# Finishing each differential head inside the next one: root, norm and turn behind the second tile

## The chip, the core and the metric

The kernel runs on one core of a Trainium2 chip. The metric is the device time of one execution in microseconds (us). Three runs of the kernel before took 1695.03, 1695.44 and 1698.78 us; the median is 1695.44. A further execution was profiled: it took 1692.59 us, of which the span of the trace covers 1690.8. All rows below are of that execution.

The engines are named as in the profile: PE is TensorE (matrix products and transposes), DVE is VectorE, ACT is ScalarE, POOL is GpSimd, SP is SyncE, which issues DMAs. Each works through its own queue of instructions.

## The reference

An encoder of two layers over 512 tokens of width 1024. Each layer has a mixer, a cross attention to 256 memory tokens and a mixture of sixteen experts, each followed by a residual and a layer norm. The mixer of the first layer is differential attention with eight heads; the change lies there:

```python
def differential_attention(x, cos, sin, w_in, lam, subln_g, w_out, lambda_init):
    h, d = DIFF_HEADS, DIFF_HEAD_DIM            # 8, 64
    q, k, v = jnp.split(x @ w_in, 3, axis=-1)
    # q, k: rope, then (seq, h, 2, d); v: (seq, h, 2 * d)
    s = jnp.einsum('bqhcd,bkhcd->bhcqk', q_blk, k)
    p = jax.nn.softmax(jnp.where(allowed, s, -jnp.inf), axis=-1)
    p_diff = p[:, :, 0] - lam_full * p[:, :, 1]
    o = jnp.einsum('bhqk,bkhe->bqhe', p_diff, v)
    o = rms_norm(o, subln_g) * (1.0 - lambda_init)
    return o.reshape(bsz, seq, h * 2 * d) @ w_out

def rms_norm(x, g):
    return x * lax.rsqrt(jnp.mean(x * x, axis=-1, keepdims=True) + LN_EPS) * g
```

A token sees the keys of its own and earlier chunks of 64. The norm is taken per token and head, over the head's 128 output columns.

## The kernel before, in words

Everything stays on one core. Weights stream from memory through a ring of buffers and are split into a high part and the rest (ScalarE writes the high part at L203 or, scaled, L207; VectorE the rest at L204 or L208). A projection is three products per chunk of 128 (`mm3`, L248 to L250).

The first mixer is a function with local helpers. `qk_proj(h)` makes queries and keys of head h: 48 products into two PSUM tiles pq, rope into two SBUF tiles qk, and for each of these two groups of four transposes, which the text calls turns: qp and kp (L430). The turned queries are evacuated to qab by ScalarE and VectorE (L253, L254), the turned keys to kS (L439, L440). `v_proj(g)` makes the values of two heads. `mem_kv(h)` makes keys and values of the memory for one head of the cross attention (mk, mv); its first call loads the memory into two tiles (L532, issued by SP) and turns it (mT, L535). These two tiles come from the same ring of two buffers as the qk tiles.

`attend(h)` goes over four tiles of 128 queries. For each: scores sc for both components (L466), mask and maximum on VectorE (L468 to L471), exponentials on ScalarE (L475), reciprocal and difference on VectorE (L478 to L481), transposes pT of the difference (L485), their copy pTs (L487), the value product po (L490). ScalarE scales po into og and, with a second pass, sums its squares into ssq (L491, L492). After the fourth tile `attend` finishes the head: twelve small VectorE instructions for the reciprocal root of ssq (`rsqrt`, L187 to L196), the scaling of og (L495), four transposes oT (L498), and the evacuation: a copy to oF for heads 0 to 5, high part and rest for heads 6 and 7 (L501, L502). When attend(6) is done, the six copies are split as well. The output projection (op0o) takes oTh and oTl.

The turns pT, qp, kp and oT and the products po share a PSUM pool of two buffers ("tp"); pq, pv, mk and mv share another of two; the scores and mT a third of two.

The driver calls qk_proj(0), v_proj(0), qk_proj(1), and then for each head attend(h) followed by the entries of a table:

```python
FILL = [["q2"], ["v1", "q3"], ["q4"], ["v2", "q5"], ["m0", "q6"], ["v3", "q7"], ["m1", "m2"], ["m3"]]
```

The order of the program text is not the order on the engines. A scheduler at build time orders the instructions of PE, DVE and ACT by its own estimate of when each could start; buffers of a pool are handed out in the order of the program text, so a turn that the text names earlier takes its buffer earlier. SP's and POOL's queues follow the text. In the result the scores of head h+1 run ahead of the end of head h, and the turns of head h+2 follow it.

At the end of the first MoE layer, ACT, DVE and the others test a register for further blocks of tokens (the branch of L1082; the trace has one such test per layer and engine, and no further block). Behind it the last expert's product is evacuated (byh, byl, L253, L254), added (mhx, L1238), and the layer norm begins (L303), which needs its gain, mg (L1221). ACT also splits weights for the second layer there, among them bwqih (L207).

Of the kernel before, what the change touches and what calls it, by code (L numbers as in the profile page):

```python
# [18 lines left out]
ALU = mybir.AluOpType  # L19
# [3 lines left out]
P = 128  # L23
D = 1024
S = 512
NT = S // P
# [3 lines left out]
EPS = 1e-5  # L30
# [35 lines left out]
def encoder(ctx: ExitStack, tc: tile.TileContext, I, out):  # L66
    nc = tc.nc
# [8 lines left out]
    def tp(name):  # L76
        return ps.tile([P, 512], F32, tag="tp", name=name, bufs=2)

    def sc2(name):
        return ps.tile([P, 1024], F32, tag="sc", name=name, bufs=2)  # L80
# [3 lines left out]
    def t4(tag, name, shape=None, dtype=F32):  # L84
        return sb.tile(shape or [P, 1024], dtype, tag=tag, name=name, bufs=BUFS[tag])

    def t2(tag, name, shape=None, dtype=F32):
        return sb.tile(shape or [P, 512], dtype, tag=tag, name=name, bufs=BUFS[tag])
# [17 lines left out]
    def small(name, shape, dtype=F32, bufs=2):  # L106
        return sb.tile(shape, dtype, tag="_" + re.sub(r"\d+", "", name), name=name, bufs=bufs)
# [4 lines left out]
    ident = const.tile([P, P], F32, name="ident")  # L112
# [70 lines left out]
    def rsqrt(x, n, name, mul, add, room=None):  # L183

        v, y, w, yi = (small(f"rs{q}{name}", [P, room or n], I32 if q == "i" else F32)[:, 0:n] for q in "vywi")
        k = 2.0 ** 26
        nc.vector.tensor_scalar(v, x, mul * k, add * k, op0=ALU.mult, op1=ALU.add)  # L187
        nc.vector.tensor_scalar(yi, v.bitcast(I32), 1, None, op0=ALU.logical_shift_right)  # L188
        nc.vector.tensor_scalar(y.bitcast(I32), yi, -1, 0x5F3759DF - 2 ** 31, op0=ALU.mult, op1=ALU.add)  # L189
        for c in (3.0, 12.0, 768.0):  # L190
            if n == 1:
                nc.vector.scalar_tensor_tensor(w, y, v, y, op0=ALU.mult, op1=ALU.mult)
            else:
                nc.vector.tensor_tensor(w, y, y, op=ALU.mult)  # L194
                nc.vector.tensor_tensor(w, w, v, op=ALU.mult)  # L195
            nc.vector.scalar_tensor_tensor(y, w, -c, y, op0=ALU.add, op1=ALU.mult)  # L196
        return y
# [44 lines left out]
    def ts(t):  # L242
        return slice(t * P, (t + 1) * P)
# [8 lines left out]
    def split_evac(hi, lo, src):  # L252
        nc.scalar.activation(hi, src, AF.Copy)  # L253
        nc.vector.tensor_sub(lo, src, hi.bitcast(F32))  # L254
# [105 lines left out]
    def diff_attention(x_ap):  # L360
# [25 lines left out]
        oF = Tall("oF", F32)  # L386
        oT = []
# [54 lines left out]
        def v_proj(g):  # L442
            W = U.get(f"wv{g}")
            vs[g] = t4("b", f"V{g}", [P, NT, 256])
            for th in range(2):
# [4 lines left out]
                        [(hT[0](k, c), hT[1](k, c), W[0][:, k, :], W[1][:, k, :]) for k in range(8)])  # L450
                nc.any.tensor_copy(vs[g][:, 2 * th:2 * th + 2, :], pv.rearrange("p (u n) -> p u n", u=2))

        def attend(h):
            V = vs[h // 2][:, :, ts(h % 2)]
            qab, K = QAB[h % 2], kS[h]
            og = t2("g", f"og{h}", [P, NT, P])
            ssq = small(f"ssq{h}", [P, NT])
            for t in range(NT):
                n = (t + 1) * P
                c = ts(t)  # L460
                nm = f"{h}{t}"
                sc = sc2(f"sc{nm}").rearrange("p (c n) -> p c n", c=2)
                w = max(n, 256)
                for cc in range(2):
                    for v in range(2):
                        nc.tensor.matmul(sc[:, cc, 0:w], qab[:, 2 * v + cc, c], K[:, cc, 0:w],  # L466
                                         start=v == 0, stop=v == 1)
                nc.vector.memset(sc[0:CHUNK, :, n - CHUNK:n], NEG)  # L468
                mx = small(f"mx{nm}", [P, 2])
                nc.vector.tensor_reduce(mx, sc[:, :, 0:n], axis=AX.X, op=ALU.max)  # L470
                nc.vector.tensor_scalar(mx, mx, -0.125, None, op0=ALU.mult)  # L471
                sm = small(f"sm{nm}", [P, 2])
                p_ = t4("c", f"p{nm}", [P, 2, 512])
                for cc in range(2):
                    nc.scalar.activation(p_[:, cc, 0:n], sc[:, cc, 0:n], AF.Exp, bias=mx[:, cc:cc + 1],  # L475
                                         scale=0.125, accum_out=sm[:, cc:cc + 1])
                rs = small(f"rs{nm}", [P, 2])
                nc.vector.reciprocal(rs, sm)  # L478
                c1 = small(f"c1{nm}", [P, 1])
                nc.vector.scalar_tensor_tensor(c1, sm[:, 0:1], rs[:, 1:2], nlam, op0=ALU.mult, op1=ALU.mult)  # L480
                nc.vector.scalar_tensor_tensor(p_[:, 0, 0:n], p_[:, 1, 0:n], c1, p_[:, 0, 0:n],  # L481
                                               op0=ALU.mult, op1=ALU.add)
                pt = tp(f"pT{nm}")
                for kt in range(t + 1):
                    nc.tensor.transpose(pt[:, ts(kt)], p_[:, 0, ts(kt)], ident)  # L485
                pT = t2("f", f"pTs{nm}")
                nc.any.tensor_copy(pT[:, 0:n], pt[:, 0:n])  # L487
                po = tp(f"po{nm}")
                for kt in range(t + 1):
                    nc.tensor.matmul(po[:, 0:P], pT[:, ts(kt)], V[:, kt, :], start=kt == 0, stop=kt == t)  # L490
                nc.scalar.activation(og[:, t, :], po[:, 0:P], AF.Copy, scale=rs[:, 0:1])  # L491
                nc.scalar.activation(junk[:, 0:P], po[:, 0:P], AF.Square, scale=rs[:, 0:1],  # L492
                                     accum_out=ssq[:, t:t + 1])
            rstd = rsqrt(ssq, NT, f"rms{h}", 1.0 / P, EPS)
            nc.vector.tensor_tensor(og, og, rstd.unsqueeze(2).to_broadcast([P, NT, P]), op=ALU.mult)  # L495
            pt = tp(f"oT{h}")
            for t in range(NT):
                nc.tensor.transpose(pt[:, ts(t)], og[:, t, :], ident)  # L498
            if oT:
                split_evac(oT[0](h), oT[1](h), pt)  # L500
            else:  # L501
                nc.any.tensor_copy(oF(h), pt)  # L502

        qk_proj(0)
        v_proj(0)
        qk_proj(1)
        for h in range(8):
            attend(h)
            if h == 6:
                for k in range(6):  # L510
                    split_evac(oT[0](k), oT[1](k), oF(k))
            for f in FILL[h]:
                if f[0] == "m":
                    mem_kv(int(f[1]))
                else:
                    (qk_proj if f[0] == "q" else v_proj)(int(f[1]))
            if h == 5:
                oT.extend((Tall("oTh"), Tall("oTl")))
        return tuple(oT)


# [1045 lines left out]
    x_ap = I["x"][0]  # L1567
    h2_d = dr.tile([S, D], F32, name="h2_d")
    oT = diff_attention(x_ap)
    nl = 2  # L1570
    for i in range(nl):
# [8 lines left out]
        oT, begun = mem_attention(i, hT)  # L1580
# [40 lines left out]
        if i + 1 < nl:  # L1621
            D3[0](DSA)
            oT = tuple(D3[1])
# [27 lines left out]
```

## Time and profile before

| what | us |
|---|---|
| runs shown, median (lowest to highest) | 1695.44 (1695.03 to 1698.78) |
| profiled execution | 1692.59 |
| its span | 1690.8 |
| PE busy in the span | 1522.3 (90%) |
| DVE busy | 1206.2 (71%) |
| ACT busy | 862.6 (51%) |

Busy time of an engine is the time in which at least one of its instructions ran. In a timeline row the first number is the start from the span's beginning, the second the duration; a bracket at the end holds the idle time of the engine ahead of it and what ended that. Matrix products are pipelined, so the duration of one reaches over the start of the next. Heads are not written in the names of a timeline; they follow from the order: the eight rows of oT at L498 are heads 0 to 7, at 100.81, 131.83, 164.67, 184.09, 212.22, 271.98, 311.54 and 330.37 us.

### The profile page before, as it was taken

The page shows a single profiled execution, that of the slowest core. Times are in us where ns is not written, and L with a number is a line of the kernel's source. Part 1 is how long each engine was busy: PE and PEld are TensorE (multiplying, and loading weights), DVE is VectorE, ACT ScalarE, POOL GpSimd, SP SyncE. Part 2 cuts the span into 40 slices and gives each one's busy share as a digit, 9 for nine tenths or more (in the row PEclk, how much of TensorE's full clock was granted, in tenths as well). Part 3 has the DMA queues.
Part 4 walks back from the last instruction along what each step waited for, and adds up shares of the span by engine and source line. Part 5 has one row for each costly group of instructions (what it writes and reads, how often), then busy time and mean ns, then how long its engine had stood idle before and what let it go on. Part 6 is the DMA issues. An engine that isn't in the chain of part 4 may idle for free. (4 is left out here: it accounts for less than half of the span.)

```text
span 1690.8 us, 23295 instructions
## 1 busy us (share of the span) xinstructions
PE 1522.3 (90%) x8572; PEld 1292.7 (76%) x8572; DVE 1206.2 (71%) x2381; ACT 862.6 (51%) x1156; POOL 230.2 (14%) x228
## 2 busy tenths in 40 slices
PE   7998799698995899999996899998998699999994
PEld 7988699597784777888875757698777487888883
DVE  5555746555447998898875698836436899899795
ACT  5443646432320775775763454533322477677671
POOL 1000000011004031231210000002002222132120
PEclk9999899799996899999997999999998699999998
DMA  7210234432415798998974301024242599899883
GB/s 227 75 51 1 75 113 157 156 91 87 165 59 213 246 364 314 311 355 314 320 254 157 96 25 63 26 89 151 76 142 110 211 363 371 281 333 368 280 300 124
DMA packets 118334, 317.58 MB, mean 188 GB/s; under 512 B 23773, under 2 KB 72925, under 8 KB 93632
## 3 DMA queue, kind: packets, MB, share of 16 engines
q1 hardware_dynamic: 100400, 272.00, 45.3%
q0 software_dynamic: 17808, 43.96, 8.5%
q8 instruction: 71, 1.16, 0.3%
q14 instruction: 55, 0.45, 0.1%
HBM read 299.38 MB, written 36.70 MB: 199 GB/s over the span
## 5 line engine op out<-in xcount | busy, mean ns | idle before, releaser
L204 DVE TENSOR_TENSOR cell_l<-cell_r,cell_h 128x2048 fp32r<-128x2048 f32 x192 | 430.7, 2285 | 40.4 <-ACT cell_h L203 39.9
L203 ACT ACTIVATE cell_h<-cell_r 128x2048 fp32r<-128x2048 f32 x192 | 363.4, 1915 | 77.7 <-DMA cell_r<-in_moe_w_up_dram 17.8
L954 PE MATMUL pg<-cell_h,xh 128*128 128x512 f32 x288 | 118.9, 413 | 2.2 <-ACT xh L253 2.2
L982 PE MATMUL py<-cell_h,hsh 128*128 128x512 f32 x288 | 115.4, 401 | 1.4 <-ACT hsh L253 0.7
L954 PE MATMUL pg<-cell_l,xh 128*128 128x512 f32 x288 | 116.2, 403 | 0.0
L982 PE MATMUL py<-cell_h,hsl 128*128 128x512 f32 x288 | 112.8, 392 | 0.0
L982 PE MATMUL py<-cell_l,hsh 128*128 128x512 f32 x288 | 112.5, 390 | 0.0
L954 PE MATMUL pu<-cell_h,xh 128*128 128x512 f32 x288 | 112.0, 389 | 0.0
L954 PE MATMUL pu<-cell_l,xh 128*128 128x512 f32 x288 | 112.0, 389 | 0.0
L972 POOL DMA_INDIRECT acc_d<-y,sx x34 | 72.9, 2143 | 152.1 <-ACT y L971 103.2
L932 POOL DMA_INDIRECT xg<-h_d,sx x32 | 42.0, 1312 | 363.8 <-DVE sx L919 334.2
L253 ACT ACTIVATE xh<-xgT 128x1024 fp32r<-128x1024 f32 x36 | 36.9, 1024 | 101.6 <-PE xgT L939 95.9
L954 PE MATMUL pg<-cell_h,xl 128*128 128x512 f32 x288 | 79.8, 400 | 0.0
L954 PE MATMUL pu<-cell_h,xl 128*128 128x512 f32 x288 | 77.0, 389 | 0.0
L954 PEld LDWEIGHTS pg<-cell_h,xh 128*128 128x128 f32 x288 | 56.6, 197 | 14.1 <-ACT xh L253 3.0
L954 PEld LDWEIGHTS pg<-cell_h,xl 128*128 128x128 f32 x288 | 56.1, 195 | 12.5
L954 PEld LDWEIGHTS pg<-cell_l,xh 128*128 128x128 f32 x288 | 56.3, 195 | 11.4
L982 PEld LDWEIGHTS py<-cell_h,hsh 128*128 128x128 f32 x288 | 54.2, 188 | 13.0 <-DVE xl L254 1.0
L982 PEld LDWEIGHTS py<-cell_h,hsl 128*128 128x128 f32 x288 | 54.0, 188 | 12.5 <-DVE hsl L254 0.4
L954 PEld LDWEIGHTS pu<-cell_h,xh 128*128 128x128 f32 x288 | 54.1, 188 | 11.2
L954 PEld LDWEIGHTS pu<-cell_h,xl 128*128 128x128 f32 x288 | 54.1, 188 | 11.2
L954 PEld LDWEIGHTS pu<-cell_l,xh 128*128 128x128 f32 x288 | 54.1, 188 | 11.2
(918 smaller groups left out, 4203.9 us busy)
## 6 DMA issues: line engine op xcount, KB each, us to landing
cell_r<-in_moe_w_gate_dram SPq DMA_DIRECT2D x64, 1024.0 KB, 7.8
cell_r<-in_moe_w_up_dram SPq DMA_DIRECT2D x64, 1024.0 KB, 7.8
cell_r<-in_moe_w_down_dram SPq DMA_DIRECT2D x64, 1024.0 KB, 6.9
mhx<-acc_d POOLq DMA_DIRECT2D x8, 512.0 KB, 7.4
x<-in_x_dram SPq DMA_DIRECT2D x4, 512.0 KB, 6.7
g<-in_ln_g_dram POOLq DMA_DIRECT2D x4, 512.0 KB, 4.0
b<-in_ln_b_dram POOLq DMA_DIRECT2D x4, 512.0 KB, 3.9
op0x<-in_x_dram POOLq DMA_DIRECT2D x4, 512.0 KB, 5.2
```

The costliest lines, as they stand in the source:

```text
L203: nc.scalar.activation(hi[:, c], raw[:, c], AF.Copy)
L204: nc.vector.tensor_tensor(lo[:, c], raw[:, c], hi[:, c].bitcast(F32), op=ALU.subtract)
L253: nc.scalar.activation(hi, src, AF.Copy)
L932: nc.gpsimd.indirect_dma_start(out=x, out_offset=None, in_=h_d[:, :], in_offset=bass.IndirectOffsetOnAxis(ap=idx[:, 0:1], axis=0), bounds_ ...
L954: nc.tensor.matmul(o, xT[l][:, a, :], W[r][:, k, :], start=a == l == r == 0, stop=a == 7 and l == 1)
L972: nc.gpsimd.indirect_dma_start(out=acc_d[:, :], out_offset=bass.IndirectOffsetOnAxis(ap=ix[:, 0:1], axis=0), in_=y, in_offset=None, bounds ...
L982: nc.tensor.matmul(o, hs[a][:, ts(2 * q + f)], Dq[b][:, f, c], start=q == f == k == 0, stop=q == f == 1 and k == 2)
```

## The change

The root, norm and turn of a head become a function of their own, `finish(h)`. It is no longer called at the end of `attend(h)` but in `attend(h + 1)`, in front of the third of its four tiles (t equal to 2). The last head is finished after the loop. og and ssq are kept in a dictionary in between. Which evacuation is taken now goes by the head's number in place of the presence of oT.

```diff
+        def finish(h):
+
+            og, ssq = ogs.pop(h)
+            rstd = rsqrt(ssq, NT, f"rms{h}", 1.0 / P, EPS)
+            nc.vector.tensor_tensor(og, og, rstd.unsqueeze(2).to_broadcast([P, NT, P]), op=ALU.mult)
+            pt = tp(f"oT{h}")
+            for t in range(NT):
+                nc.tensor.transpose(pt[:, ts(t)], og[:, t, :], ident)
+            if h > 5:
+                split_evac(oT[0](h), oT[1](h), pt)
+            else:
+                nc.any.tensor_copy(oF(h), pt)
+
         def attend(h):
             V = vs[h // 2][:, :, ts(h % 2)]
             qab, K = QAB[h % 2], kS[h]
             og = t2("g", f"og{h}", [P, NT, P])
             ssq = small(f"ssq{h}", [P, NT])
+            ogs[h] = og, ssq
             for t in range(NT):
+                if t == 2 and h:
+                    finish(h - 1)
                 n = (t + 1) * P
...
                 nc.scalar.activation(junk[:, 0:P], po[:, 0:P], AF.Square, scale=rs[:, 0:1],
                                      accum_out=ssq[:, t:t + 1])
-            rstd = rsqrt(ssq, NT, f"rms{h}", 1.0 / P, EPS)
-            nc.vector.tensor_tensor(og, og, rstd.unsqueeze(2).to_broadcast([P, NT, P]), op=ALU.mult)
-            pt = tp(f"oT{h}")
-            for t in range(NT):
-                nc.tensor.transpose(pt[:, ts(t)], og[:, t, :], ident)
-            if oT:
-                split_evac(oT[0](h), oT[1](h), pt)
-            else:
-                nc.any.tensor_copy(oF(h), pt)
-
+
+        ogs = {}
         qk_proj(0)
...
             if h == 5:
                 oT.extend((Tall("oTh"), Tall("oTl")))
+        finish(7)
         return tuple(oT)
```

The order on the engines at three places, of before and of the change. The rows give line, operation, output and inputs; a number behind a name tells tiles apart, and x4 stands for four of the same in a row. Lines of the change are shifted (oT L498 is L460, sc L466 is L482, pT L485 is L501, po L490 is L506, mT L535 is L544).

On PE at the end of head 1, before: po_1072 is that head's last value product, sc_1445 the scores of the last tile of head 2, qp and kp the turns of head 3, pv the values of heads 4 and 5.

```order
L490 MATMUL po_1072<-V_419,pTs_1070 128x128 x4
L466 MATMUL sc_1445<-kS_818,qab_268 128x512 x4
L498 MATMUL oT_1096<-ident,og_961 128x128 x4
L430 MATMUL qp_1323<-ident,qk_1315 128x128 x4
L430 MATMUL kp_1330<-ident,qk_1315 128x128 x4
L430 MATMUL qp_1345<-ident,qk_1337 128x128 x4
L430 MATMUL kp_1352<-ident,qk_1337 128x128 x4
L248 MATMUL pv_1797<-wv2h,xTh_127 128x256
```

The same place with the change:

```order
L506 MATMUL po_1072<-V_419,pTs_1070 128x128 x4
L430 MATMUL qp_1300<-ident,qk_1292 128x128 x4
L482 MATMUL sc_1445<-kS_795,qab_268 128x512 x4
L430 MATMUL kp_1307<-ident,qk_1292 128x128 x4
L430 MATMUL qp_1322<-ident,qk_1314 128x128 x4
L430 MATMUL kp_1329<-ident,qk_1314 128x128 x4
L248 MATMUL pv_1774<-wv2h,xTh_127 128x256
```

oT of head 1 has left this place; the first qp now stands ahead of the scores, and the turns follow the value product.

On PE at the end of head 3, before: po_1760 is its last value product, oT_1784 its turn, qp and kp are the turns of head 5, pT_2067 and what follows belong to head 4.

```order
L485 MATMUL pT_1753<-ident,p_1745 128x128 x4
L466 MATMUL sc_2103<-kS_1506,qab_268 128x384 x4
L490 MATMUL po_1760<-V_1108,pTs_1758 128x128 x4
L466 MATMUL sc_2133<-kS_1506,qab_268 128x512 x4
L498 MATMUL oT_1784<-ident,og_1649 128x128 x4
L430 MATMUL qp_2011<-ident,qk_2003 128x128 x4
L430 MATMUL kp_2018<-ident,qk_2003 128x128 x4
L430 MATMUL qp_2033<-ident,qk_2025 128x128 x4
L430 MATMUL kp_2040<-ident,qk_2025 128x128 x4
L485 MATMUL pT_2067<-ident,p_2059 128x128
L490 MATMUL po_2071<-V_1796,pTs_2069 128x128
L485 MATMUL pT_2093<-ident,p_2085 128x128 x2
```

With the change:

```order
L501 MATMUL pT_1753<-ident,p_1745 128x128 x4
L506 MATMUL po_1760<-V_1085,pTs_1758 128x128 x4
L430 MATMUL qp_1988<-ident,qk_1980 128x128 x4
L482 MATMUL sc_2133<-kS_1483,qab_268 128x512 x4
L430 MATMUL kp_1995<-ident,qk_1980 128x128 x4
L430 MATMUL qp_2010<-ident,qk_2002 128x128 x4
L430 MATMUL kp_2017<-ident,qk_2002 128x128 x4
L501 MATMUL pT_2044<-ident,p_2036 128x128
L506 MATMUL po_2048<-V_1773,pTs_2046 128x128
L501 MATMUL pT_2070<-ident,p_2062 128x128 x2
L544 MATMUL mT_2169<-ident,mem_2167 128x128 x8
L506 MATMUL po_2075<-V_1773,pTs_2073 128x128 x2
```

The turns of head 5 stand directly behind the value product; the next row after these twelve is oT of head 3 (oT_2097), behind the second value product of head 4. In the same order the turns of head 4 stand ahead of the last products of head 5's projection, where before they stood behind them.

On ACT at the end of the first MoE layer, before, up to the branch and behind it:

```order
L971 ACTIVATE y_14_8122<-py_14_8097,sw_14_7665 128x1024
L253 ACTIVATE hsh_15_8158<-hT_15_8153 128x512
L203 ACTIVATE bwqh<-bwqr 128x512 x4
L203 ACTIVATE bwkvh<-bwkvr 128x512 x4
L1082 COMPARE_AND_BRANCH
...
L253 ACTIVATE byh_9220<-py_15_8162 128x512 x2
L207 ACTIVATE bwqih<-bwqir,gq 128x1024 x2
```

With the change:

```order
L980 ACTIVATE y_14_8122<-py_14_8097,sw_14_7665 128x1024
L253 ACTIVATE hsh_15_8158<-hT_15_8153 128x512
L203 ACTIVATE bwqh<-bwqr 128x512 x4
L203 ACTIVATE bwkvh<-bwkvr 128x512 x4
L207 ACTIVATE bwqih<-bwqir,gq 128x1024 x2
L1091 COMPARE_AND_BRANCH
```

The two weight copies bwqih have moved ahead of the branch, and so ahead of byh. The queues of SP and POOL keep their order.

## Rows read from the trace of the kernel before

**Rows 1.** The page, busy time, share of the span and instructions of two engines.

```profile
PE 1522.3 (90%) x8572; PEld 1292.7 (76%) x8572; DVE 1206.2 (71%) x2381; ACT 862.6 (51%) x1156; POOL 230.2 (14%) x228
```

**Rows 2.** What PE waited for from 0 to 345 us: line, releaser, total us, times, longest.

```profile
PE oT L498 <- DVE og L495: 17.7, 4, 4.6
...
PE kp L430 <- DVE kS L440: 3.9, 2, 3.5
```

**Rows 3.** Timeline of PE at the ends of head 0 and head 1.

```profile
100.81 0.60 PE L498 MATMUL oT<-ident,og 128*128 128x128 f32 x4
101.25 0.60 PE L430 MATMUL qp<-ident,qk 128*128 128x128 f32 x4
...
103.31 0.66 PE L430 MATMUL qp<-ident,qk 128*128 128x128 f32 x4 [0.55 <-DVE qab L254]
107.43 0.66 PE L430 MATMUL kp<-ident,qk 128*128 128x128 f32 x4 [3.47 <-DVE kS L440]
...
125.25 1.05 PE L490 MATMUL po<-V,pTs 128*128 128x128 f32 x8
126.06 1.17 PE L466 MATMUL sc<-kS,qab 128*128 128x512 f32 x4
131.83 0.72 PE L498 MATMUL oT<-ident,og 128*128 128x128 f32 x4 [4.60 <-DVE og L495]
132.34 1.06 PE L430 MATMUL qp<-ident,qk 128*128 128x128 f32 x4
...
136.44 0.35 PE L248 MATMUL pv<-wv2h,xTh 128*128 128x256 f32 x1
```

**Rows 4.** Busy time by stretch: the stretch, its length, busy us and instructions of PE, PEld, DVE, ACT and POOL, the granted clock of PE as a share of full speed, DMA share, GB/s.

```profile
108.00:112.00 4.00, 3.98 (x22) 3.92 (x21) 2.56 (x7) 1.30 (x2) 0.00 (x0) 0.57 0.96 261
...
132.00:136.00 4.00, 3.53 (x18) 2.67 (x17) 1.65 (x4) 2.59 (x5) 0.00 (x0) 0.57 0.00 0
...
169.00:180.00 11.00, 7.52 (x46) 5.85 (x46) 9.25 (x33) 9.06 (x32) 0.00 (x0) 1.00 0.00 1
180.00:184.00 4.00, 0.00 (x0) 0.00 (x0) 3.63 (x14) 0.00 (x0) 0.00 (x0) 0.93 0.00 0
184.00:202.00 18.00, 14.00 (x66) 11.92 (x67) 10.86 (x19) 13.99 (x29) 0.00 (x0) 0.64 0.19 63
...
303.00:320.00 17.00, 9.87 (x36) 7.90 (x37) 14.05 (x44) 9.40 (x31) 1.05 (x2) 0.50 0.62 219
```

**Rows 5.** Timeline of ACT and DVE at the end of head 7: the last og, and the first and the last of the thirteen instructions of DVE that finish the head.

```profile
326.41 0.37 ACT L491 ACTIVATE og<-po,rs 128x128 f32<-128x128 f32 x1 [1.25 <-PE po L490]
...
327.16 0.17 DVE L187 TENSOR_SCALAR rsvrms<-ssq 128x4 f32<-128x4 f32 x1 [5.54 <-ACT junk L492]
...
329.53 0.69 DVE L495 TENSOR_TENSOR og<-og,rsyrms 128x512 f32<-128x512 f32 x1
```

**Rows 6.** Timeline of PE from the last product of head 5's queries and keys to the first product of mk that others follow.

```profile
166.14 0.28 PE L250 MATMUL pq<-wqk5h,xTl 128*128 128x256 f32 x1
...
169.47 0.33 PE L485 MATMUL pT<-ident,p 128*128 128x128 f32 x1 [0.53 <-DVE qab L254]
...
172.31 0.68 PE L490 MATMUL po<-V,pTs 128*128 128x128 f32 x4
...
177.40 1.16 PE L490 MATMUL po<-V,pTs 128*128 128x128 f32 x8
...
184.09 1.09 PE L498 MATMUL oT<-ident,og 128*128 128x128 f32 x4 [4.57 <-DVE og L495]
...
201.76 0.39 PE L249 MATMUL mk<-memTl,mwk0h 128*128 128x256 f32 x1 [0.53 <-DVE memTl L254]
```

**Rows 7.** Timeline of SP: the issue of the memory's two loads.

```profile
187.03 2.87 SPq L532 DMA_DIRECT2D mem<-in_mem_dram  x2
```

**Rows 8.** Timeline of PE from the last product of mk3 to the turn of head 7: mk3's and mv3's last products, the value product of head 7's second tile, its turn.

```profile
290.52 0.28 PE L250 MATMUL mk<-memTh,mwk3l 128*128 128x256 f32 x1
...
297.52 0.28 PE L250 MATMUL mv<-mwv3h,memTl 128*128 128x256 f32 x1
...
318.57 1.05 PE L490 MATMUL po<-V,pTs 128*128 128x128 f32 x4
...
330.37 1.08 PE L498 MATMUL oT<-ident,og 128*128 128x128 f32 x4 [4.00 <-DVE og L495]
```

**Rows 9.** Timeline of ACT: a pair of weight copies for the output projection, and an exponential of 384 columns.

```profile
301.74 0.89 ACT L207 ACTIVATE op0w10h<-op0w10r,gsub 128x256 fp32r<-128x256 f32 x2
...
313.19 0.57 ACT L475 ACTIVATE p<-sc,mx 128x384 f32<-128x384 f32 x1
```

**Rows 10.** Timelines of ACT and DVE at the end of the first MoE layer, and of the instructions at L1082 (duration in ns, lowest, median and highest, over both layers) one of POOL's.

```profile
887.82 0.60 ACT L253 ACTIVATE byh<-py 128x512 fp32r<-128x512 f32 x1 [1.98 <-PEq L1082]
...
893.44 2.19 ACT L207 ACTIVATE bwqih<-bwqir,gq 128x1024 fp32r<-128x1024 f32 x2 [3.61 <-DMA bwqir<-in_b_w_qidx_dram]
...
893.33 1.28 DVE L1238 SCALAR_TENSOR_TENSOR mhx<-pc,pw,mhx 128x1024 f32<-128x1024 f32 x1 [0.71 <-DMA mhx<-acc_d]
...
902.73 1.28 DVE L303 SCALAR_TENSOR_TENSOR mhx<-mhx,mn,mg 128x1024 f32<-128x1024 f32 x1 [7.92 <-DMA mg<-in_ln_g_dram]
...
L1082 POOLq EVENT_SEMAPHORE  x10: 17/43/5637, 875.8 to 1657.9; - x10
```

## Prediction

> **What bounds the kernel now.** I read the page's share of busy time first. TensorE is busy 90% of the span and VectorE 71% [rows 1], so the idle tenth of TensorE is all that a pure reordering can win, and it counts only where TensorE then goes on with work that is waiting. Next I read what TensorE waited for in the first 345 us, where the eight differential heads lie [rows 2]. The turn oT (L498) heads the list: 17.7 us in four waits on VectorE's og (L495), 4.4 us each. The reader is to see that four of eight turns wait and the other four do not.
>
> Why, the timeline shows. Behind the turn of head 1 no product of a projection is left in TensorE's queue: the turn waits 4.60 us at 131.83, and the four turns qp and kp of head 3 follow it [rows 3]. At head 0 the turn itself has no wait, yet it has taken a buffer of the PSUM pool that the turns use, and the kp turn that follows waits 3.47 us at 107.43. After such a pause the granted clock falls: in 108 to 112 TensorE is busy 3.98 of 4 us at 0.57, in 132 to 136 for 3.53 us at 0.57, in 184 to 202 for 14.00 us at 0.64, in 303 to 320 for 9.87 us at 0.50 [rows 4]. Of the two levels, 2.4 and 1.2 GHz, these are stretches mostly or wholly at the lower. So a wait costs itself and part of the work behind it.
>
> **What each turn waits for.** At head 7 ScalarE scales the last tile of og at 326.41 and squares it; then thirteen VectorE instructions stand in a row, 327.16 to 330.22, with nothing between [rows 5]. That is 3.8 us alone; the longest wait of rows 2, 4.6, and the 0.9 of the value product ahead make 5.5 where other VectorE work lies between. This chain moves; its length stays.
>
> **The change, part by part.** No instruction is added or removed: the chain, the four transposes and the copy of each head stand behind tile 1 of the next head. After the last value product of a head TensorE now goes straight to the qp and kp turns of the head after next (the order shown above, end of head 1). Those take 4.10 us from 132.34 to 136.44 [rows 3], and the tiles 0 and 1 of the next head stand between, which took 3.5 us for head 3 (169.47 to 172.99) [rows 6]. 7.6 us exceed 5.5, so oT should find og ready. If that cover were gone, 4.4 us per head come back, in another place.
>
> *First stretch, heads 0 to 2 (100 to 166 us) [rows 3, 4].* Head 0: the 3.47 us should go, as the turns no longer stand behind oT in the pool, and with it the clock loss of 108 to 112, 4 x 0.43 = 1.7; the 0.55 of qp for its evacuation stays. Together 5.2. Head 1: before, value product to first V product takes 125.25 to 136.44, 11.2. Now it is 0.8 for the product, 0.9 for the scores (1.17 with what overlaps the next), 4.1 for the four turns, 5.8: a gain of 5.4. Against it, three turns of head 4 at 0.44 (the oT at 100.81 to the qp behind it) and a pT of some 0.15 less an oT of 0.44, 1.0, now stand ahead of the stretch's end, and I take 0.5 off for kp, which still shares VectorE with the split of a weight. Sum 9.1. Bounds: 4.1 (the 4.60 alone, less that 0.5) and 12.3 (waits 0.55 + 3.47 + 4.60 + 0.5, clock 1.7 + 0.43 x 3.53).
>
> *Second stretch, no projection left (from the last product of head 5's, 166.42, to the first run of mk, 201.76: 35.3 us) [rows 6].* The turns of head 4 now lie under head 5's products: 166.42 to 169.47, 3.05, and the first pT another 0.7 sooner. The memory load: SP issues it at 187.03 [rows 7], when the tiles of qk, whose buffers it takes, have been turned, 8.5 us behind the end of the value product (177.40 + 1.16). The new order puts qp and kp directly behind that product, with the scores between (the order shown above, end of head 3): 0.5 + 0.9 + 0.9, 2.3 us; gain 6.2. From the issue to mk is 14.7 now; one oT moves inside it and waits less, 0.9. Head 3's chain from its pT to its last value product, 9.1, gets oT of head 2 inside, minus 0.7. Sum 10.2; I take 8.5, since the low clock of 184 to 202 remains at least in part. Bounds: 4.6 (the wait at 184.09 alone) and 16.5 (idle 3.48 + 4.00 + 4.00 in 169 to 202, clock 0.36 x 14.00 = 5.0) [rows 4].
>
> *Third stretch, the tail (last product of mk3 at 290.80 to oT of head 7 at 330.37: 39.6 us) [rows 8].* Head 7's own wait of 4.00 stays. oT of head 6 loses its wait, about 4.5, in front of the tiles of head 7. But the order puts sixteen of ScalarE's weight copies (L207) between og of head 6 and og of head 7's first tile; a pair takes 0.80 (0.89 with what overlaps the next) [rows 9], so 6.4. New working: the products of mv3 end 10.2 after 290.80 in place of 7.0 (297.80), as 3.2 us more of head 6's and 7's turns, value and score products stand between. Then 0.7 of og and Square, 1.1 of two exponentials (0.57 each for 384 columns), 6.4 of copies, 0.7 of og for tile 0 of head 7, 2.5 of VectorE, turn and product of tile 1: oT of head 6 11.4 later, at +21.6. Two tiles of head 7 follow, 9.9 (318.57 to 330.37 takes 11.8, of which some 1.9 are output products at the low clock), and 1.3 for output products that moved ahead. 32.8: a gain of 6.8. I take 5.0, as these copies are the part least sure. Bounds: 0 (oT's wait comes back behind the copies) and 12.0 (idle 7.13 and clock 0.5 x 9.87 in 303 to 320) [rows 4].
>
> *The end of the first MoE layer.* The scheduler moved two weight copies of ScalarE (bwqih, L207) ahead of the branch for further blocks, so byh waits for their load. Before, byh ran at 887.82 and bwqih at 893.44 for 2.19 [rows 10]: byh comes at 895.6, 7.8 later, and the second mhx, which ended at 894.61, at 902.4. The layer norm's first step (L303) waits for mg until 902.73: covered by 0.3, cost 0. If the cover is gone the excess is paid: up to 3.1, if the branch on ScalarE then holds as long as the longest on POOL, 5.64 us (893.4 + 5.6 = 899.0, 3.4 past 895.6, less the 0.3). The Trainium skill, "Runtime: NRT & Kernel Launch", section "Instruction fetch mechanics", says that a taken branch whose target lies outside the fetched window waits for a fetch; by it the sum loses those 3.1. POOL's 5.64 agrees with it, its median of 0.043 in the same row does not.
>
> All else keeps its order but for some neighbours; TensorE is dense there and I count 0, give or take 3.
>
> *Sum:* 9.1 + 8.5 + 5.0 = 22.6 of the profiled execution's 1692.6 (span 1690.8 and 1.8 around it): 1670.0. The median of the runs shown, 1695.4, is 2.8 above the profiled one, so 1672.8: 1673.
>
> **The rivals.**
> 1. *Only the waits go.* The oT waits but head 7's vanish (17.7 - 4.0 = 13.7) and neither the clock, kp's wait, nor the memory load follows: 1695.4 - 13.7 = 1681.7. For it: the lower clock in those stretches also lies beside exponentials and evacuations that stay. Against it: the load is tied to the turns that move up.
> 2. *Slower: oT in the middle of the next head holds TensorE.* TensorE works in order, so an oT whose og is late stops the next head's tiles 2 and 3. Price at most 4.4 x 7 = 31, against 13.7 + 3.47 = 17.1 saved: 1695.4 + 14 = 1709. It decides from a mean wait of 2.45 us per head. For it: VectorE's chain now competes with the next head's maxima and sums. Against it: 7.6 us of cover against 5.5.
> 3. *The branch on ScalarE exposes its fetch.* Forecast plus 3.1: 1675.9. For it: one branch of 5.64 us in the row; against it: the cover by mg.
> 4. *No change:* the waits come back one for one, as the first kp wait did for oT's at head 0 (3.47 against 4.6): 1695. Against it: at the second stretch no work stands in front of the freed engine that could absorb all of it.
>
> **How the numbers follow.** The forecast has 0.62, rival 1 0.20, rival 3 0.08, rival 4 0.05, rival 2 0.05. The likeliest's own range is 1665 to 1681. The whole: low bounds 4.1 + 4.6 + 0 = 8.7 saved, less 3.1, so 1689.8; high bounds 40.8, of which I let 33 count: 1662. I state 1662 to 1688. Runs of this kernel tell apart about 0.2%, 3.4 us. Faster holds the forecast, rivals 1 and 3: 0.62 + 0.20 + 0.08 less 0.02 of their edges, 0.88; the same 0.06; slower 0.06.
>
> **What the profile after would show.** Right: the oT row of TensorE's waits falls from 17.7 to the 4 us of head 7; qp follows head 1's last value product within 1 us; SP issues the memory load about 2.5 us after head 3's last value product; head 7's oT lies some 22 us earlier, and the distance from it to the end is that of before. Step one is wrong if kp still waits for kS at head 0's end; step two if the load still comes 8 us after the product; step three if oT of head 6 waits behind ScalarE's copies. The forecast as a whole is wrong if oT waits for og in the middle of heads, or if the time won by 345 us is lost again at the MoE layer's end.

## The result and the profile after

The changed kernel took 1672.54 us (median of four runs, 1672.02 to 1678.64), the kernel before 1696.12 in the same comparison (1695.03 to 1698.78). The ratio is 0.9866, 95% interval 0.985 to 0.9882: 23.6 us faster, 1.3%. The forecast was 1673, from a sum of 22.6 us. The profiled execution's span went from 1690.8 to 1670.5 us.

The page, the same line as [rows 1]:

```profile
PE 1516.7 (91%) x8572; PEld 1290.8 (77%) x8572; DVE 1202.6 (72%) x2379; ACT 863.5 (52%) x1158; POOL 232.1 (14%) x228
```

TensorE has the same 8572 products and 5.6 us less busy time, in line with a mean granted clock of 0.953 over the span in place of 0.950; the rest of the 20.3 us is idle time that is gone.

What PE waited for from 0 to 330 us (line, releaser, total, times, longest), against [rows 2]:

```profile
PE oT L460 <- DVE og L457: 11.0, 2, 7.0
...
PE mk L248 <- ACT memTh L253: 1.8, 1, 1.8
...
PE pT L501 <- DVE qab L254: 1.5, 1, 1.5
...
PE pv L248 <- ACT qk L410: 1.3, 1, 1.3
...
PE kp L430 <- DVE kS L440: 0.7, 2, 0.3
```

Of the four waits of oT two are left, heads 6 and 7, and the one at head 6 has grown to 7.0 us. The wait of kp for kS has shrunk from 3.5 to 0.3. Three small waits are new or longer (mk for memTh, pT for qab, pv for qk): the next things in line.

Timeline of PE at the end of head 1, against [rows 3]:

```profile
118.91 1.06 PE L506 MATMUL po<-V,pTs 128*128 128x128 f32 x8
119.81 0.60 PE L430 MATMUL qp<-ident,qk 128*128 128x128 f32 x4
120.16 1.17 PE L482 MATMUL sc<-kS,qab 128*128 128x512 f32 x4
121.17 0.60 PE L430 MATMUL kp<-ident,qk 128*128 128x128 f32 x4
122.35 0.65 PE L430 MATMUL qp<-ident,qk 128*128 128x128 f32 x4 [0.58 <-DVE qab L254]
123.34 0.66 PE L430 MATMUL kp<-ident,qk 128*128 128x128 f32 x4 [0.33 <-DVE kS L440]
125.33 0.35 PE L248 MATMUL pv<-wv2h,xTh 128*128 128x256 f32 x1 [1.34 <-ACT qk L410]
...
134.65 0.60 PE L460 MATMUL oT<-ident,og 128*128 128x128 f32 x4
```

From the value product to the first V product it is now 6.42 us (118.91 to 125.33), before 11.19. The reader should look at the durations too: a turn of four lasts 0.60 to 0.66 here, before 1.06. The last row is the moved oT: 15.7 us behind the value product, without a wait.

Busy time by stretch, columns as in [rows 4]: the end of head 1, the second stretch in two parts, and the tail.

```profile
118.00:125.00 7.00, 5.08 (x38) 4.14 (x36) 5.28 (x17) 4.68 (x13) 0.00 (x0) 1.00 0.00 0
...
171.00:180.00 9.00, 6.24 (x36) 5.54 (x36) 7.28 (x21) 7.57 (x18) 0.00 (x0) 0.81 0.17 56
180.00:187.00 7.00, 4.98 (x25) 4.60 (x26) 5.68 (x8) 4.73 (x11) 0.00 (x0) 0.76 0.49 160
...
297.00:309.00 12.00, 7.09 (x35) 6.26 (x35) 3.62 (x15) 3.06 (x9) 1.05 (x2) 0.64 0.69 237
```

At head 1 the granted clock stays at its upper level (1.00, before 0.57) although 1.9 of the 7 us are idle in pieces. The second and third rows here are the later part of the second stretch, as the row of 0.64 in [rows 4] was. Over the whole stretch, from the last product of head 5's projection to the run of mk, the mean granted clock is 0.90 (156 to 185 us), before 0.81 (166 to 202); from the last product of mk3 to the turn of head 7 it is 0.85 (275 to 309), before 0.78 (290 to 331).

The second stretch on PE, against [rows 6]:

```profile
156.44 0.28 PE L250 MATMUL pq<-wqk5h,xTl 128*128 128x256 f32 x1
...
164.59 1.16 PE L506 MATMUL po<-V,pTs 128*128 128x128 f32 x8 [0.68 <-ACT pTs L503]
...
169.19 0.66 PE L430 MATMUL kp<-ident,qk 128*128 128x128 f32 x4 [0.33 <-DVE kS L440]
171.31 0.33 PE L501 MATMUL pT<-ident,p 128*128 128x128 f32 x1 [1.46 <-DVE qab L254]
...
173.77 1.91 PE L544 MATMUL mT<-ident,mem 128*128 128x128 f32 x8
...
176.07 0.60 PE L460 MATMUL oT<-ident,og 128*128 128x128 f32 x4
...
180.60 0.38 PE L248 MATMUL mk<-memTh,mwk0h 128*128 128x256 f32 x1 [1.81 <-ACT memTh L253]
```

and SP's issue of the memory's loads, against [rows 7]:

```profile
167.63 2.63 SPq L541 DMA_DIRECT2D mem<-in_mem_dram  x2
```

The run of mk that [rows 6] end with starts at 184.93: 28.5 us from the last product of head 5's projection, before 35.6. oT of head 3 stands between the two runs of mT, without a wait. SP issues 1.9 us behind the end of the value product (165.75), before 8.5. But from that issue to mk it is 17.3 us, before 14.7. Of the 2.6 more, 0.9 lie ahead of the first mT (6.1 us behind the issue, before 5.3) and 1.8 between the first mk and its run (4.3 us, before 2.5), where a value product and a turn of head 4 now stand; from the first mT to the first mk it is as long as before (6.8 and 6.9).

The tail on PE, against [rows 8]:

```profile
284.90 0.28 PE L250 MATMUL mv<-mwv3h,memTl 128*128 128x256 f32 x1
287.18 0.39 PE L506 MATMUL po<-V,pTs 128*128 128x128 f32 x2
...
297.42 1.09 PE L460 MATMUL oT<-ident,og 128*128 128x128 f32 x4 [7.04 <-DVE og L457]
...
308.22 1.09 PE L460 MATMUL oT<-ident,og 128*128 128x128 f32 x4 [4.00 <-DVE og L457]
```

oT of head 7 comes 22.15 us earlier than before (330.37). That is nearly all of the 23.6 us of the timed runs, so the gain is made by here.

The end of the first MoE layer on ACT, against [rows 10]:

```profile
865.97 2.19 ACT L207 ACTIVATE bwqih<-bwqir,gq 128x1024 fp32r<-128x1024 f32 x2 [3.95 <-DMA bwqir<-in_b_w_qidx_dram]
868.41 0.60 ACT L253 ACTIVATE byh<-py 128x512 fp32r<-128x512 f32 x1 [0.25 <-ACTq L1091]
```

and on DVE:

```profile
878.36 1.28 DVE L303 SCALAR_TENSOR_TENSOR mhx<-mhx,mn,mg 128x1024 f32<-128x1024 f32 x1 [3.15 <-DMA mg<-in_ln_g_dram]
```

The moved copies wait 3.95 us for their load and byh comes behind them; the layer norm still waits for mg, 3.15 us in place of 7.92. In this execution the cover held. In a second profile of the same kernel (the changed kernel once more, below) it did not:

```profile
875.17 2.19 ACT L207 ACTIVATE bwqih<-bwqir,gq 128x1024 fp32r<-128x1024 f32 x2 [9.55 <-SPq L1091]
877.61 0.60 ACT L253 ACTIVATE byh<-py 128x512 fp32r<-128x512 f32 x1 [0.25 <-ACTq L1091]
```

```profile
884.34 1.28 DVE L303 SCALAR_TENSOR_TENSOR mhx<-mhx,mn,mg 128x1024 f32<-128x1024 f32 x1
```

There the copies start 10.6 us behind the issue of their load (4.9 in the first profile), and the layer norm starts without a wait for mg: the chain behind byh is what holds it. From hsh of the last expert to the layer norm it is 23.48 us, against 21.10 in the first profile and 21.65 before.

### The profile page after: what moved, and what is told of

It is laid out like the page before. It is cut to its first block, busy times and chain, and to the rows that moved or that the text cites. A ratio compares the mean times of both kernels' runs of the same rounds, so it can differ in the third digit from the quotient of the medians.

```text
span 1670.5 us, 23288 instructions
## 1 busy us (share of the span) xinstructions
PE 1516.7 (91%) x8572; PEld 1290.8 (77%) x8572; DVE 1202.6 (72%) x2379; ACT 863.5 (52%) x1158; POOL 232.1 (14%) x228
## 5 line engine op out<-in xcount | busy, mean ns | idle before, releaser
L991 PEld LDWEIGHTS py<-cell_l,hsh 128*128 128x128 f32 x288 | 54.6, 190 | 10.6
```

What stands on the lines that cost most here:

```text
L991: nc.tensor.matmul(o, hs[a][:, ts(2 * q + f)], Dq[b][:, f, c], start=q == f == k == 0, stop=q == f == 1 and k == 2)
```

## The experiments

Theory A: a finish holds TensorE, and the turns that stand behind it, at its own place; taken away from there, the gain is local, and gains add up. The rivals were that the memory load is the whole gain (B), that only the named waits count (C), that VectorE's relief at the boundary is what counts (D), and the slower case of the prediction.

**One group of heads at a time.** In `attend`, with D = [0, 1, 2], [3, 4, 5] or [6]; all other heads (7 apart, which stays behind the loop) are finished behind their own fourth tile:

```diff
-                if t == 2 and h:
+                if t == 2 and h - 1 in D:
                     finish(h - 1)
...
+            if h not in D and h < 7:
+                finish(h)
```

> Only heads 0 to 2 are finished inside the next head; heads 3 to 6 are finished at their own end as before. Theory A (each finish holds TensorE and the turns behind it at its own place, so the gains are local and add up): the 9.7 us that the changed kernel had won by the last product of head 5's projection, nothing further: about 1686.4, and the waits of oT at heads 3 and 6 (4.6, 4.5) are there. Rival B (the gain is one thing, the memory load that starts sooner): under 3 us, about 1694. Rival C (only the waits of oT and kp themselves count, 4.6 + 3.5): 8.1, 1688.

> Only heads 3 to 5 are finished inside the next head. Theory A: 166.4 to 201.8 gets shorter by 4 to 8 us (the changed kernel won 7.1 there, but 3 of it came from turns of head 4 that now lie behind head 2's finish again), about 1690; the memory load is issued 2 us behind head 3's last value product. Rival B (the load is the whole gain): 15 or more, below 1681. Rival C: 4.6 alone, 1691.5, with the load still 8 us behind.

> Only head 6 is finished inside the next head. Theory A: the tail from the last product of mk3 to oT of head 7, 39.6 us before, gets 7 shorter, about 1689, although oT of head 6 then waits some 7 us for og. Rival C (only waits count): oT of head 6 waits longer than the 4.5 it did, so nothing is won or 2.5 us are lost, 1696 to 1698.

Measured: 1684.08 us (ratio 0.9922, 0.99 to 0.9943), 1687.33 (0.994, 0.9917 to 0.9964) and 1690.96 (0.9956, 0.9944 to 0.9968), beside 1697.58 for the kernel before on that chip. The three gains of the timed runs add up to 30.4 us (13.5, 10.3, 6.6), more than the changed kernel's 23.6, so the totals don't tell which part won what. The starts of the same instructions in each profile tell where a gain arises. All in us: the first column is a start from the span's beginning, the others are differences of starts.

| finished in the next head | last product of head 5's q and k | from there to the run of mk | to the last product of mk3 | to oT of head 7 |
|---|---|---|---|---|
| none (before) | 166.14 | 35.62 | 88.76 | 39.85 |
| 0 to 2 | 158.73 | 33.69 | 88.76 | 40.21 |
| 3 to 5 | 166.00 | 30.49 | 91.81 | 32.40 |
| 6 | 166.63 | 35.59 | 88.11 | 34.86 |
| 0 to 6 (the change) | 156.44 | 28.49 | 90.49 | 32.80 |

A second profile of the changed kernel (below) repeats its last three columns to 0.01 us and has 157.50 in the first. In the second stretch the gains add up to a tenth: 1.93 + 5.13 + 0.03 = 7.09, and the change won 7.13. Rival B falls: heads 0 to 2 alone win 9.0 us by oT of head 7 and leave the load where it was, 8.5 us behind the value product. The waits of oT that are left within the first 345 us show the same, one row of each kernel (heads 0 to 2, then 3 to 5):

```profile
PE oT L460 <- DVE og L457: 13.1, 3, 4.6
```

```profile
PE oT L460 <- DVE og L457: 14.0, 3, 5.4
...
PE kp L430 <- DVE kS L440: 4.2, 3, 3.5
```

The wait of kp at head 0 is still there (3.5) when head 0 is finished at its own end. In the last two columns theory A's adding up fails. From the run of mk to oT of head 7, heads 3 to 5 alone win 4.40 us and head 6 alone 5.64, but the change wins 5.32, not 10.0. And heads 3 to 5 alone shorten the tail by 7.45 us although head 6 is finished at its own end and its oT waits 5.4. In that kernel nothing of head 6 but its oT stands behind the last product of mv3; before, its last two value products did. So in that kernel the tail is shorter because more of head 6 has run under the products of mk and mv when these run out. With head 6 alone, its last two value products still stand behind mv3 (297.53), and the tail is 4.99 us shorter in place of the 7 expected; oT of head 6 waits 1.69 us there, not 7. The two ways of shortening the tail overlap: together, in the change, they win no more of it than heads 3 to 5 alone.

**Root and norm back at the head's end.** Only the turn and its copy stay behind the second tile of the next head:

```diff
         def finish(h):
 
             og, ssq = ogs.pop(h)
-            rstd = rsqrt(ssq, NT, f"rms{h}", 1.0 / P, EPS)
-            nc.vector.tensor_tensor(og, og, rstd.unsqueeze(2).to_broadcast([P, NT, P]), op=ALU.mult)
             pt = tp(f"oT{h}")
...
                                      accum_out=ssq[:, t:t + 1])
+            rstd = rsqrt(ssq, NT, f"rms{h}", 1.0 / P, EPS)
+            nc.vector.tensor_tensor(og, og, rstd.unsqueeze(2).to_broadcast([P, NT, P]), op=ALU.mult)
```

> The changed kernel, but root and norm stand at the head's own end again; only the turn and its copy stand behind the second tile of the next head. Theory A (TensorE's place of the turn is what counts): as the changed kernel within 2 us, 1672 to 1675. Rival D (the gain comes from VectorE, whose thirteen instructions no longer stand between the scores and evacuations at the boundary): half of the gain or more is lost, 1684 or above.

Measured: 1676.42 us, ratio 0.9878 (0.9857 to 0.9899); oT of head 7 at 310.25, 20.1 of the 22.15 us. A little above theory A's range, far from rival D's: TensorE's place of the turn is what counts. (The turn's place in TensorE's queue and its place in the PSUM pool moved together; no run separates the two.) In this kernel the two weight copies bwqih stand behind the branch again, as in all the others but the changed one:

```profile
876.06 2.19 ACT L207 ACTIVATE bwqih<-bwqir,gq 128x1024 fp32r<-128x1024 f32 x2 [5.67 <-SPq L1091]
```

They start 10.7 us behind the issue of their load (865.38); the profile names SP at its own branch as the releaser, as in the second profile of the changed kernel. Before, it was 8.6 us (884.83 to 893.44); in the other ten experiments it is 9.4 to 10.5. Only the first profile of the changed kernel has 4.9.

**Another tile of the next head.** `t == 1` and `t == 3` in place of `t == 2`.

> Each head is finished behind the first tile of the next head instead of the second. Theory A: the cover shrinks from the turns and two tiles (7.6 us by the forecast) to the turns and one tile, some 5.6, against 5.5 that og needs where VectorE has other work; so oT waits 0 to 2 us at heads 1 and 3, and the first tile of head 7 no longer lies ahead of oT of head 6: 1673 to 1679. Rival E (any place behind the boundary does the same): 1671 to 1674, without a new wait for og.

> Each head is finished behind the third tile of the next head. Theory A: more cover than is needed at heads 0 to 5, so nothing changes there; at head 6 the 7.0 us that oT waits for og are partly filled by the third tile of head 7: 1668 to 1673. Rival F (the turn now meets the end of the next head, where pT, po and the next turns want the same PSUM buffers): waits of kp or qp come back at heads 0 to 3 and it is slower than 1676.

Measured: 1672.93 us (0.9864, 0.9842 to 0.9886) and 1668.66 (0.9843, 0.982 to 0.9866). Behind the first tile no wait for og came back at heads 0 to 5, so rival E was right and my measure of the cover too short: in the changed kernel oT of head 3 starts 11.5 us behind its head's last value product (164.59 to 176.07), not 7.6. Behind the first tile the second stretch is longer all the same, 31.9 us against 28.5. Behind the third tile oT of head 6 waits for nothing; the row of the waits is down to head 7:

```profile
PE oT L460 <- DVE og L457: 3.7, 1, 3.7
```

But a part of the wait has only changed its place. A turn pT of head 7, which now stands ahead of oT, waits 3.0 us for VectorE, which at that time also works off weight splits of the output projection and the root of head 6:

```profile
295.50 0.66 PE L501 MATMUL pT<-ident,p 128*128 128x128 f32 x2 [3.03 <-DVE rsyrms L189]
```

**A longer chain.** Twelve copies of the sum of squares, one after the other, ahead of each root; they change no value:

```diff
+            for _ in range(12):
+                ss2 = small(f"ssc{h}", [P, NT])
+                nc.vector.tensor_scalar(ss2, ssq, 1.0, None, op0=ALU.mult)
+                ssq = ss2
             rstd = rsqrt(ssq, NT, f"rms{h}", 1.0 / P, EPS)
```

> The order of before (each head finished at its own end), with twelve more VectorE instructions of 0.2 us in front of each root, which copy the sum of squares and change nothing: the chain is 2.4 us longer. Theory A: the four waits of oT (heads 1, 3, 6, 7) each grow by 2.4: 9.6 slower than before, about 1706, and the head 0, 2, 4, 5 turns show none. If VectorE's own load counts (8 x 2.4 = 19): 1715.

> The changed kernel with the same twelve instructions in front of each root. Theory A (the chain lies under the turns and the first two tiles of the next head, except for head 7 and partly head 6): 2.4 at head 7, 0 to 2.4 at head 6, at most 1 each at heads 1 and 3: 1675 to 1679. Rival (the slower case of the prediction: an oT in the middle of a head holds TensorE): 2.4 at all eight heads, 1690 or above.

Measured: 1708.06 us (1.006, 1.0036 to 1.0084), 10.8 slower than before, and 1674.88 (two runs only; 0.9874, 0.9853 to 0.9896), whose interval overlaps that of the changed kernel. The waits, to 350 us, of the order of before with the longer chain:

```profile
PE oT L464 <- DVE og L461: 27.3, 4, 7.0
```

and of the changed kernel with it:

```profile
PE oT L464 <- DVE og L461: 16.5, 3, 9.4
```

27.3 - 17.7 = 9.6 = 4 x 2.4: before, every microsecond of the chain is paid at four heads. In the changed kernel heads 6 and 7 pay 2.4 each (7.04 to 9.41, 4.00 to 6.46), head 2 pays 0.61, the others nothing. The slower case, oT holding TensorE in the middle of each head, is ruled out; it holds at head 6 alone.

**Ranking on one chip, and the memory load.** The changed kernel and `t == 3` once more; a mixed one with head 6 behind the third tile and heads 0 to 5 behind the second; and the order of before with the first half of the memory loaded into half tiles that are free by then:

```diff
-            mt = t4("d", f"mem{u}")
-            nc.sync.dma_start(mt, I["mem"][0, u * P:(u + 1) * P, :])
+            mt = [t2("e", f"mem{u}{z}") for z in range(2)] if u == 0 else t4("d", f"mem{u}")
+            for z in range(2 - u):
+                if u == 0:
+                    nc.sync.dma_start(mt[z], I["mem"][0, 0:P, z * 512:(z + 1) * 512])
+                else:
+                    nc.sync.dma_start(mt, I["mem"][0, P:2 * P, :])
```

> The changed kernel once more, on the chip and in the rounds of the next three, so that they can be ranked against it: 1672 to 1674, 22 to 25 below the kernel before.

> Every head finished behind the third tile of the next head, once more beside the changed kernel. If the 3.9 us between the two medians so far are real, 1667 to 1670; if they are the spread of chips and rounds, within 1.5 us of the changed kernel.

> Heads 0 to 5 finished behind the second tile, head 6 behind the third tile of head 7. Theory A (the gains are local and add up): the first 275 us as the changed kernel, the tail as with the third tile everywhere (29.85 us from the last product of mk3 to oT of head 7 in place of 32.8): 3 us below the changed kernel, about 1669.5. If the gain of the third tile is that of all heads together: as the changed kernel, 1672.5.

> Each head is finished at its own end, as before; the first half of the memory is loaded into two free half tiles instead of a qk tile, so that SP can issue its load some 20 us sooner, and the second half takes the qk buffer that comes free first. If the load is what the second stretch waited for (the term of 6.2 us in the forecast): 4 to 6 us faster, about 1690 to 1692. If the load is covered, and TensorE's turns stand where they stand because of oT and the turns ahead of them: within 1.5 us of before.

Measured, beside 1696.64 for the kernel before: the changed kernel 1676.25 us (0.9873, 0.9855 to 0.9891), above the 1672 to 1674 expected, the third tile 1669.61 (0.9848, 0.9835 to 0.9861), mixed 1671.08 (0.9854, 0.9838 to 0.987), the memory early 1697.65 (1.0005, 0.9994 to 1.0017).

The third tile was ahead of the changed kernel both times, by 3.9 us across two comparisons and by 6.6 within one. Not all of that comes from the heads: in the profiles of the second comparison the stretch from hsh of the last expert to the layer norm is 23.48 us in the changed kernel and 21.05 with the third tile, which has bwqih behind the branch. How much is the tile's own stays open: its two profiles have oT of head 7 at 309.38 and 305.27, the changed kernel's two at 308.22 and 309.29. The tail from mk3 is shorter in both (29.85 and 28.88, against 32.80 in both). The mixed one is 5.2 us below the changed kernel in the timed runs, with 3 expected; but its tail from the last product of mk3 is 31.32, only 1.5 shorter, and 2.3 us of the rest arise at the end of the MoE layer (21.16 us there). So the local tail carries over only in part, and the timed gap does not show that it does.

The early load won nothing: from the last product of head 5's projection to the run of mk it is 36.7 us there, before 35.6. SP's issues there:

```profile
108.00 1.15 SPq L544 DMA_DIRECT2D mem<-in_mem_dram  x2
189.37 0.33 SPq L546 DMA_DIRECT2D mem<-in_mem_dram  x1
```

and the turn of the first half on PE:

```profile
194.06 1.91 PE L549 MATMUL mT<-ident,mem 128*128 128x128 f32 x8
```

The first half is issued at 108 in place of 187 us and its turn still comes at 194 (192.32 before): it stands where it does because of what is ahead of it in TensorE's queue. Only the first half was tested so: the second is issued at 189.37, as before (189.6), but it lands 3.5 us later, ahead of its turn at 196.62.

## Why the prediction was right, step by step

*Sum.* 22.6 us forecast, 23.6 timed, 22.15 by oT of head 7 in the two profiles. The terms were 9.1, 8.5 and 5.0. Measured: 9.70, 7.13, then 1.73 lost under the products of mk (88.76 to 90.49), a term that the forecast did not have, and 7.05 won in the tail. So the parts are off by 0.6, -1.4, -1.7 and 2.1 us, and the sum by 0.45: that it fits so closely is partly luck. Two of the forecast's own signs spoke against it: the row of oT's waits fell to 11.0, not to the 4 of head 7, and oT of head 6 waits behind ScalarE's copies, by which its step three was to be wrong.

*First stretch: right in mechanism and size.* The wait of kp at head 0 went, the clock stayed up, and head 1's end takes 6.42 us against the 5.8 worked out; it has a new wait of the V product, 1.34 us for ScalarE's copy of qk, which frees the PSUM tile it writes. The forecast put the wait of kp down to the pool. The row before shows what stood in the way on VectorE: kS of that kp had its ScalarE half done at 104.82 and started at 106.68, behind the split of a weight.

```profile
104.36 2.29 DVE L204 TENSOR_TENSOR wqk5l<-wqk5r,wqk5h 128x2048 fp32r<-128x2048 f32 x1 [1.11 <-ACT wqk5h L203]
```

With the change the four turns of head 2 start at 90.66 in place of 101.25, directly behind head 0's last value product and with products of a projection between them, so TensorE has no wait there. How much of this the pool does is not shown. The experiment with heads 0 to 2 alone shows that it is these heads that win it: 7.4 of the 9.7; by the other two alone 0.1 and -0.5. The other 2.6 belong to no single group, and 1.1 of them is what two profiles of one kernel differ by here.

*Second stretch: right in sign, wrong in its cause.* The failing step is "The memory load: ... gain 6.2" and "From the issue to mk is 14.7 now; one oT moves inside it and waits less, 0.9". The load did come sooner, by 6.6 us, but it was no limit: with its first half issued 79 us sooner nothing was won, and the turns of the memory (mT) wait for it neither there nor before. It had little to spare, though: before, it landed 3.5 us behind its issue, 1.8 us ahead of its turn. Had it stayed 8.5 us behind the value product, it would have held the turns back in the changed kernel (an estimate: 165.75 + 8.5 + 3.5 = 177.7, the turn starts at 173.77). From its issue to mk the time grew by 2.6 in place of shrinking by 0.9. What went is oT with its 4.57 in front of the four turns of head 5: from the end of the value product to the start of the last kp it is 3.4 us (165.75 to 169.19). Before, it was 9.8 us, from 178.56 to this row:

```profile
188.38 1.12 PE L430 MATMUL kp<-ident,qk 128*128 128x128 f32 x4
```

The first product of mk then waits 1.81 us for its evacuation. On ACT the second half of memTh stands behind a weight copy and behind the copy oF of the moved oT:

```profile
177.23 1.92 ACT L203 ACTIVATE mwk0h<-mwk0r 128x2048 fp32r<-128x2048 f32 x1
179.03 0.59 ACT L464 COPY oF<-oT 128x512 f32<-128x512 f32 x1
179.50 1.05 ACT L253 ACTIVATE memTh<-mT 128x1024 fp32r<-128x1024 f32 x1
```

So a part of what left the boundary stands in the way 10 us later: 0.59 of it is the moved head's own copy.

*Third stretch: right in size, half right in mechanism.* "oT of head 6 loses its wait" is wrong: it waits 7.04, more than before. The forecast's own working had it late, behind ScalarE's sixteen copies, and that is what happened:

```profile
286.00 3.30 ACT L207 ACTIVATE op0w01h<-op0w01r,gsub 128x256 fp32r<-128x256 f32 x8
289.20 3.30 ACT L207 ACTIVATE op0w10h<-op0w10r,gsub 128x256 fp32r<-128x256 f32 x8
292.39 0.35 ACT L507 ACTIVATE og<-po,rs 128x128 f32<-128x128 f32 x1
```

6.4 us for both as worked out (292.39 - 286.00), and oT of head 6 12.2 us behind the end of mv3 (285.18), 11.4 worked out. The tail is shorter because fewer tiles are left in it, which heads 3 to 5 alone also bring (7.45). The working had this too: it put oT of head 6 at 21.6 us behind the last product of mk3, and it came at 21.7. Its 6.8 met the 7.05 measured; taking 5.0 of it was needless caution.

*The MoE boundary: right in the first profile, and there by luck.* The forecast put byh 14.5 us behind hsh of the last expert, with 0.3 us of cover left, and the cost at 0. It came 11.15 us behind in the first profile, with 3.15 us left, and 16.75 behind in the second, with nothing left (before 6.74). The difference is the load of the moved copies: 4.9 us from its issue to their start in the first profile, 10.6 in the second, 8.6 to 10.7 in every other one. Without cover, from hsh to the layer norm is 23.48 us, against 21.05 to 22.50 in the eleven experiments that have the copies behind the branch: the move then costs some 1 to 2.4 us. The term "cost 0" is therefore not safe. How often the load comes early, two profiles don't tell.

*The rivals.* Only the waits (1681.7): ruled out, 13.7 us by that, 23.6 measured, though oT's waits fell by 6.7 only; and the clock at head 1's end stayed up. Slower through oT in the middle: ruled out by the longer chain. The branch on ScalarE: byh waited 0.25 us for it in both profiles, so its price was not there; what uncovered the layer norm in the second profile was the wait of the copies ahead of the branch. The 5.64 us of POOL that this rival leans on belong to an EVENT_SEMAPHORE at the branch's line, and no run shows what it waited for. No change: ruled out.

## What to carry to other kernels

When an in-order engine waits at the end of each round of a loop for a chain on another engine, move the instruction that waits behind work of the next round that does not need it; what matters is its place in the waiting engine's queue and in the pool that it shares (the two moved together here), not where the chain is computed. Check the move by lengthening the chain: before, it was paid at four heads in full, afterwards in full only at the last two, where too little work or none stands in front of the turn. Look also at what the build's scheduler moved elsewhere: here two weight copies far behind the change went ahead of an evacuation that needs no load. A transfer that starts later for the same reason as everything else is a symptom; issue it sooner by itself before you book its time as a gain.

## What was not expected of the chip

Two profiled executions of one and the same program, the changed kernel, differ by 5.3 us in span (1670.5 and 1675.8). They are 1.07 apart at oT of head 7, 4.1 at the first layer norm behind the cross attention (491.37 and 495.48), 3.6 at hsh of the last expert of the first MoE layer (857.26 and 860.86), 9.2 at byh (868.41 and 877.61) and 6.0 at the layer norm behind it (878.36 and 884.34). So 3.0 arise between the heads and that first layer norm, for a reason that was not looked for, and 2.4 at the end of the MoE layer, where the load of bwqih was late the second time.

The starts within the heads are not always closer than the totals. The two profiles of the third tile differ by 4.1 us at oT of head 7 (309.38 and 305.27), 2.8 of it in the second stretch (30.62 and 27.81 us), and by 3.5 in span (1666.7 and 1663.2). A gain of 3 us in this program needs both: the starts, which tell where it arises, and more than one profile.
